# Storing the first tile later and the last tile in two pieces, in a one-core SiLU-times-gate kernel

## Chip, cores, metric

One core of one Trainium2 chip. The metric is device time in microseconds (us); lower is better. Times inside a run are counted from the start of its span, as the profile gives them.

## The reference

The input is `x`, float32 of shape 32 x 512 x 2048. Each row is split in half; the output, 32 x 512 x 1024 float32, is `silu(first half) * second half`:

```python
half_dim = x.shape[-1] // 2
x1, x2 = x[..., :half_dim], x[..., half_dim:]
return (x1 * (1 / (1 + np.exp(-x1))) * x2).astype(np.float32)
```

So 134.2 MB are read and 67.1 MB written, with two operations per output element.

## The kernel before

The 16,384 rows are cut into 16 tiles of 8 rows on each of 128 partitions. Loads go out from SP, stores from ACT, each tile in one transfer: 8.4 MB in, 4.2 MB out. The silu runs on ACT, the product on DVE. Two input and two output buffers. Only the first tile (in chunks of 2 rows) and the last (stored in four pieces of 2 rows) are treated differently.

```python
K = 8
KC_EDGE = 2
# ... pools of 2 buffers each; silu() on ACT and mul() on DVE over rows c to ce ...
def load(i):
    xt = in_pool.tile([P, K, in_cols], dt, name="xt")
    nc.sync.dma_start(out=xt[:, :plan[i][1], :], in_=view(x_flat, i))
    loaded[i] = xt

load(0)
load(1)
for i in range(n_tiles):
    xt = loaded.pop(i)
    ov = view(out_flat, i)
    ot = out_pool.tile([P, K, half], dt, name="ot")
    if i < n_tiles - 1:
        kc = KC_EDGE if i == 0 else K
        for c in range(0, K, kc):
            silu(ot, xt, c, c + kc)
            mul(ot, xt, c, c + kc)
        nc.scalar.dma_start(out=ov, in_=ot)
        if i + 2 < n_tiles:
            load(i + 2)
        continue

    cuts = list(range(0, K, KC_EDGE))
    for n, c in enumerate(cuts + [None, None]):
        if c is not None:
            silu(ot, xt, c, c + KC_EDGE)
            mul(ot, xt, c, c + KC_EDGE)
        if n >= 2:
            b = cuts[n - 2]
            nc.scalar.dma_start(out=ov[:, b:b + KC_EDGE, :], in_=ot[:, b:b + KC_EDGE, :])
```

## Time and profile before

| | before |
|---|---|
| time, median of 3 runs | 470.57 us (470.44 to 471.02) |
| span of the profiled run | 468.6 us |
| DVE / ACT busy | 30% / 24% |
| bytes moved, mean rate | 201.3 MB, 430 GB/s |
| tile 0 done on DVE, store 0 issued | 32.7 us |
| last load lands | 450.65 us |
| store 14 lands; last piece lands | 457.9; 467.7 us |

Read it from the DMA side: the 16 DMA engines (here "engines", where nothing else is said) are busy throughout, and the compute engines wait for them. The lines that show this stand in the prediction.

### The profile page before, as it was taken

How to read it: one execution, taken by the hardware profiler on the slowest of the kernel's cores; microseconds unless marked ns; L12 is line 12 of the kernel's file. 1: busy time of each engine (PE TensorE's matmuls, PEld its weight loads, DVE VectorE, ACT ScalarE, POOL GpSimd, SP SyncE). 2: the span in 40 equal slices, each digit the busy share in tenths (PEclk: the TensorE clock that was granted, in tenths of full speed). 3: DMA queues.
4: the chain of work that ended last, by engine and by line, in shares of the span. 5: the costliest groups of instructions: out<-in, count | busy, mean ns of one | idle time of the engine just before them, and what ended most of it. 6: DMA issues, size and time to landing. Idle time of an engine off the chain costs nothing.

```text
span 468.6 us, 183 instructions
## 1 busy us (share of the span) xinstructions
DVE 139.5 (30%) x22; ACT 114.3 (24%) x23; POOL 0.2 (0%) x4
## 2 busy tenths in 40 slices
DVE  0070510606115060250702407024070330703333
ACT  1141405023050230503205032050410504105050
POOL 0000000000000000000000000000000000000000
DMA  9899999999999998998999999999999999999998
GB/s 442 386 425 403 439 456 448 403 417 434 448 448 403 448 470 380 448 481 380 481 400 420 478 448 403 403 448 448 448 403 445 434 420 448 431 420 492 394 411 358
DMA packets 5040, 201.33 MB, mean 430 GB/s; under 512 B 560, under 2 KB 560, under 8 KB 560
## 3 DMA queue, kind: packets, MB, share of 16 engines
q1 hardware_dynamic: 2304, 134.22, 66.4%
q10 hardware_dynamic: 2736, 67.11, 33.2%
HBM read 134.22 MB, written 67.11 MB: 430 GB/s over the span
## 4 chain that ended last, share of the span: by engine, by line
DMA 72%; DVE 14%; ACT 11%; DVEq 0%; issue 0%; ACTq 0%
DMA xt<-in_x_dram 72%; DVE ot L85 14%; ACT ot L78 11%; DVEq L140 0%; ACTq L78 0%
## 5 line engine op out<-in xcount | busy, mean ns | idle before, releaser
L85 DVE TENSOR_TENSOR ot<-ot,xt 128x8192 f32<-128x8192 f32 (+1 forms) x22 | 139.5, 6362 | 322.1 <-ACT ot L78 322.1
L78 ACT ACTIVATE ot<-xt 128x8192 f32<-128x8192 f32 (+1 forms) x22 | 113.0, 5163 | 343.0 <-DMA xt<-in_x_dram 343.0
L78 ACT ACT_TABLE_LOAD x1 | 1.3, 1283 | 0.8 <-PEq L129 0.8
L129 POOL MEMSET const-bfloat16-1.0<- 128x1 bf16 x1 | 0.1, 101 | 0.0
L129 POOL MEMSET const-uint8-127<- 128x1 uint8 x1 | 0.1, 101 | 0.0
L129 POOL MEMSET const-float32-0.0<- 128x1 f32 x1 | 0.1, 98 | 0.2 <-issue 0.2
L129 POOL MEMSET const-float32-1.0<- 128x1 f32 x1 | 0.1, 98 | 0.0
## 6 DMA issues: line engine op xcount, KB each, us to landing
out_dram<-ot ACTq DMA_DIRECT2D x15, 4096.0 KB, 34.7
out_dram<-ot ACTq DMA_DIRECT2D x4, 1024.0 KB, 5.7
xt<-in_x_dram SPq DMA_DIRECT2D x16, 42.1
```

The costliest lines, as they stand in the source:

```text
L78: nc.scalar.activation(out=ot[:, c:ce, :], in_=xt[:, c:ce, :half], func=mybir.ActivationFunctionType.Silu,)
L85: nc.vector.tensor_mul(out=ot[:, c:ce, :], in0=ot[:, c:ce, :], in1=xt[:, c:ce, half:],)
L129: nc = _bacc.Bacc("TRN2", target_bir_lowering=False, num_devices=1)
```

## The change

Its intent: with tile 0 in chunks of 4, 2 and 2 its store is issued later, so the loads get ahead of the stores; the last tile is then computed sooner and can be stored in two larger pieces without the queue running dry.

```diff
+    KS = 4
+    CHUNKS_FIRST = [4, 2, 2]
@@ tiles 0 to 14
-            kc = KC_EDGE if i == 0 else K
-            for c in range(0, K, kc):
+            c = 0
+            for kc in CHUNKS_FIRST if i == 0 else [K]:
                 silu(ot, xt, c, c + kc)
                 mul(ot, xt, c, c + kc)
+                c += kc
@@ last tile (the old loop over cuts is removed)
+        pieces = []
+        for c in range(0, K, KC_EDGE):
+            silu(ot, xt, c, c + KC_EDGE)
+            if len(pieces) == 1 and c == K - KC_EDGE:
+                nc.scalar.dma_start(out=ov[:, pieces[0]], in_=ot[:, pieces[0]])
+            mul(ot, xt, c, c + KC_EDGE)
+            if (c + KC_EDGE) % KS == 0:
+                pieces.append(slice(c + KC_EDGE - KS, c + KC_EDGE))
+        nc.scalar.dma_start(out=ov[:, pieces[-1]], in_=ot[:, pieces[-1]])
```

More of the change, by code (lines that the diff above doesn't have):

```diff
@@ L105 @@
             continue
-        cuts = list(range(0, K, KC_EDGE))
-        for n, c in enumerate(cuts + [None, None]):
-            if c is not None:
-                silu(ot, xt, c, c + KC_EDGE)
-                mul(ot, xt, c, c + KC_EDGE)
-            if n >= 2:
-                b = cuts[n - 2]
-                nc.scalar.dma_start(out=ov[:, b:b + KC_EDGE, :], in_=ot[:, b:b + KC_EDGE, :])
+        pieces = []
[7 more added lines that the diff above has]
+        nc.scalar.dma_start(out=ov[:, pieces[-1]], in_=ot[:, pieces[-1]])
 _INS = ['x']
```

## The prediction

> **What bounds the kernel now.** I read the page first, for which resource is busy.
>
> ```profile
> span 468.6 us, 183 instructions
> DVE 139.5 (30%) x22; ACT 114.3 (24%) x23; POOL 0.2 (0%) x4
> ...
> DMA  9899999999999998998999999999999999999998
> ...
> q1 hardware_dynamic: 2304, 134.22, 66.4%
> q10 hardware_dynamic: 2736, 67.11, 33.2%
> HBM read 134.22 MB, written 67.11 MB: 430 GB/s over the span
> ```
>
> The reader is to see two engines idle for 70% and more, and a row of nines: the transfers fill the span. q1 (loads) and q10 (stores) together take 99.6% of the 16 DMA engines. Next, the same by stretch, cut at the first load's data, the first store, the last load's landing and the end of the data (the last two columns are DMA share and GB/s):
>
> ```profile
> 2.00:21.80 19.80, 0.00 (x0) 0.06 (x1) 0.00 (x0) 1.00 0.98 424
> ...
> 38.80:450.60 411.80, 121.69 (x14) 98.41 (x14) 0.00 (x0) 1.00 1.00 434
> 450.60:457.90 7.30, 5.23 (x3) 7.17 (x4) 0.00 (x0) 1.00 0.95 410
> 457.90:467.40 9.50, 3.67 (x2) 0.14 (x1) 0.00 (x0) 1.00 0.95 403
> 467.40:468.63 1.23, 0.00 (x0) 0.00 (x0) 0.00 (x0) 1.00 0.00 0
> ```
>
> A packet counts in the window in which it starts, hence the wobble in short ones. Third, the chain of waits, at its start and end:
>
> ```profile
> 44.84 7.04 ACT ot L78
> 51.88 0.02 issue
> 51.90 8.70 DVE ot L85
> 60.61 0.02 issue
> 60.62 42.14 DMA xt<-in_x_dram
> ...
> 450.73 1.92 ACT ot L78
> 452.65 0.02 issue
> 452.67 6.70 DVE ot L85 x3
> 459.37 2.20 DVEq L140
> ```
>
> It alternates ACT 7.04, DVE 8.70 and a load of 42.1 us, and so looks like a dependency loop. It is not one: the load issued at 60.6 stands in the queue behind another that takes the first 13 us, so shortening ACT or DVE would only lengthen its wait. The packet records confirm this: from 1.0 us to the last data at 467.4 no DMA engine pauses, with one exception given below. The end is therefore the start of the data, plus the sum of the packets' times, plus any gap in the feeding.
>
> Fourth, the tail in the timeline:
>
> ```profile
> 450.73 5.51 ACT L78 ACTIVATE ot<-xt 128x2048 f32<-128x2048 f32 x3 [21.93 <-DMA xt<-in_x_dram]
> 452.67 8.90 DVE L85 TENSOR_TENSOR ot<-ot,xt 128x2048 f32<-128x2048 f32 x4 [15.15 <-ACT ot L78]
> 455.00 0.34 ACTq L114 DMA_DIRECT2D out_dram<-ot  x1
> 456.15 1.89 ACT L78 ACTIVATE ot<-xt 128x2048 f32<-128x2048 f32 x1
> 457.20 4.74 ACTq L114 DMA_DIRECT2D out_dram<-ot  x3
> ```
>
> The four pieces of the last store are issued at 455.00, 457.20, 459.4 and 461.6, and take 5.4, 5.6, 5.9 and 6.1 us to land: at 460.4, 462.8, 465.3 and 467.7, a steady 2.44 us apart (1.05 MB in 2.44 us is 430 GB/s). Store 14, issued at 437.56, lands 20.4 us later at 457.9. So the pieces wait behind it, and the queue is full until the last byte. The first piece has 457.0 - 455.0 = 2.0 us of slack before the first engine is done with store 14 (packet records: engines finish it between 456.96 and 457.56).
>
> **What the Trainium skill says.** "DMA: Bandwidth & Descriptors", section "Queues, rings and completion order": each DMA engine goes round-robin between the queue rows that have work, a packet at a time. The trace agrees. Load packets are 65,536 B and take 2.418 us, store packets 32,768 B and take 1.213 us, and they alternate on each engine, which gives 134.22 to 67.11 MB, two to one. The same page, section "Issuing engines are not separate DMA queues", says that transfers from different issuing engines share the same 16 DMA engines; the 66.4% and 33.2% that add to one budget show it. "Perfetto Trace Analysis", section "DMA Instruction — HWDGE (DVE, Sync)", says that the profiled window of such an issue leaves out the data movement: here 0.34 us of issue against 5.4 to 6.1 us to landing. The same page, section "DMA Optimizations", recommends larger transfers for throughput but splitting where some part can then start sooner. The change trades one against the other.
>
> **The change part by part.**
>
> *1. Fewer, larger pieces.* Each engine moves 32 packets of 8,192 B in the tail now: 32 x 0.309 = 9.89 us. It will move 16 packets of 16,384 B. Between 8,192 B (0.309) and 32,768 B (1.213) the line is 0.3013 us per 8 KiB plus 0.008 per packet, so a 16 KiB packet should take 0.610 (an estimate), and 16 of them 9.77. Saved: 0.12 us, and two completion records of 0.01 us: 0.14 us in all. This is on the path that sets the end, because the queue is.
>
> *2. Tile 0 in 4, 2, 2.* Four 128x2048 activations take 7.31 us, one 1.893, one of 128x8192 7.029. By the line between the sizes a 128x4096 one takes 3.61. On DVE 2.286 and 8.692 give 4.42 for 128x4096. Tile 0 lands at 21.83: first silu to 25.44, first mul 25.47 to 29.89, then two of 2 rows at 2.21 apart, the last ending at 34.30. Now it ends at 32.67. Store 0 and load 2 go out 1.63 us later, at 34.33. Load 2 loses nothing, since load 1 keeps the queue busy to 44.8. Store 0 enters the alternation later, so all loads move ahead of the stores. With smooth sharing they would land 1.63/2 = 0.8 us earlier. In truth it goes by packets: an engine either fits in one more load packet before its first store packet, and then every load is ahead by one store packet, 1.21 us, or it does not and nothing moves. Total bytes are unchanged, so this part alone moves the end by 0; its use is to start the last tile's computing sooner.
>
> Which is it? Store 0, issued at 32.70, has its first packet at 38.86 to 39.46, after load packets that began at 33.0 and 35.5. The latter took 3.4 instead of 2.42 us: that is the exception, a 1.0 us pause as the idle store queue wakes. An engine starts a load packet every 2.42 us, so the latest issue that still gets this slot lies somewhere between 32.70 (which got it) and about 34.6 (one packet time later, less the 0.5 us by which the engines differ); where, the records do not say. 34.33 is near the far end, so a shift is likelier than not, but the first load got its data only 1.0 us after its issue, which would put the limit late. I give 60% to the whole shift, 15% to only some engines shifting (a load lands when its slowest engine does, so that is worth little), 25% to none.
>
> *3. The tail's feeding.* The first piece now needs four rows, so it waits for the second mul: 457.20, not 455.00. With the shift it is 457.20 - 1.21 = 455.99. The second and last goes out at 461.61, or 460.40 shifted. From issue to data flowing on idle engines I take the first load: issued at 0, its first packets start at 1.00 to 1.74, but the second ones only at 4.03 to 4.55; less one packet of 2.42, data flow counts as starting 1.6 to 2.1 us after the issue.
> - Shifted: ready at 457.6 to 458.1, against engines that run dry at 456.96 to 457.56. A gap of about 0.5 us; less the 0.14 saved, +0.4 us. The second piece is ready at 460.40 + 2.1 = 462.5, before the first is done at 457.9 + 4.9 = 462.8: no second gap, barely.
> - Not shifted: ready at 458.8 to 459.3, a gap of some 1.8 us, less 0.14: +1.6 to +1.7 us.
>
> The last landing is followed by about 0.9 us of ending that stays.
>
> **The rivals.**
> - *A hidden tail*: the shift happens and a busy queue takes up a new store without a pause. Speaking for it: stores 1 to 14 queue behind one another and no pause shows. Against: they are issued some 5 us before they are needed (store 13 takes 34.7 us to land, of which 29 are its own share), this piece 1 us. Then only -0.14 remains: 470.4.
> - *A bare tail*: no shift, gap in full. For it: 34.33 is close to the old slot. 472.2.
> - *A new buffer wait*: a later store 0 could hold up the output buffer, of which there are two. Store 13 lands at 443.4 and tile 15 starts to write the same buffer at 450.7: 7.3 us of slack. The store is later by 2.4 at most, the load earlier by 1.2: 3.7 us remain. Unlikely.
> - *Compute-bound end*: the last mul ends at 461.6 in both, earlier with the shift, and cannot set the end alone.
>
> **Range and chances.** The time of a run is about 2.0 us above the trace's span, 470.57 against 468.6, which I hold constant. 60% near 471.0 (470.57 + 0.4), 25% near 472.2, the rest between, with the hidden tail at the low side and 0.3 us of run noise (470.44 to 471.02 before): 471.0, range 470.0 to 472.4. Two per cent is 9.4 us, more than any term here; it would take a steady stall that I do not see. Faster 0.5%, same 98.5%, slower 1%.
>
> **What would show each step.** Right: tile 0's last DVE instruction ends near 34.3 and store 0 is issued just after; later loads land 1.2 us earlier than now (load 15 at 449.4 rather than 450.65); the two last issues are 4.4 us apart near 456.0 and 460.4; store 14 still lands near 457.9; the DMA rate between 38.8 and 449 stays 434 GB/s. Wrong: load 15 still at 450.65 (no shift), a pause of over 1 us in the store queue after store 14, a 16 KiB packet that is not near 0.61 us, or ACT waiting for an output buffer. The forecast as a whole fails if the span moves by more than 2 us, which would mean that the alternation itself has a different rhythm.

## More of the kernel before

One more view is needed. A count of the packets that start between 38 and 41 us shows when store 0 gets its turn (columns: packets, MB, share of the 16 engines; q1 is the loads' queue, q10 the stores'):

```profile
DMA packets 32, 1.57 MB, mean 524 GB/s; under 512 B 0, under 2 KB 0, under 8 KB 0
...
q1 hardware_dynamic: 16, 1.05, 80.6%
q10 hardware_dynamic: 16, 0.52, 40.4%
```

All 16 engines start exactly one store packet here. I call this the early slot of store 0.

## The result, and the profile after

| | before, same rounds | changed |
|---|---|---|
| median | 470.66 us (6 runs) | 471.53 us (6 runs) |
| range | 470.44 to 471.02 | 470.42 to 472.30 |
| the runs | 470.57, 471.02, 470.44, 470.56, 470.90, 470.75 | 470.42, 472.30, 472.12, 472.18, 470.62, 470.94 |

A ratio here is the mean time of one kernel's fast runs over the mean of the other's of the same rounds, so not quite the ratio of the medians. It is 1.0015 (95% interval 0.9998 to 1.0033): the same, within 2%. But the changed kernel has two modes: three runs at 470.4 to 470.9 and three at 472.1 to 472.3. All runs are with the clock at 1.0.

The profiled run is the one of 470.42. Its page, against the lines of before in the prediction:

```profile
span 468.5 us, 179 instructions
...
q1 hardware_dynamic: 2304, 134.22, 66.5%
q10 hardware_dynamic: 2448, 67.11, 33.2%
```

Four instructions and 288 store packets fewer (2,736 before), the same bytes, the same span to 0.1 us. The stretches, cut at this run's own marks (last columns: DMA share, GB/s):

```profile
41.30:449.50 408.20, 121.70 (x14) 98.41 (x14) 0.00 (x0) 1.00 1.00 434
449.50:458.00 8.50, 6.43 (x3) 7.31 (x4) 0.00 (x0) 1.00 0.97 418
458.00:467.40 9.40, 2.47 (x2) 0.00 (x0) 0.00 (x0) 1.00 0.94 403
```

The long middle still moves 434 GB/s. The chain of waits and the tail of the timeline:

```profile
43.59 7.04 ACT ot L80
...
50.65 8.70 DVE ot L87
...
59.37 42.20 DMA xt<-in_x_dram
```

```profile
449.63 7.31 ACT L80 ACTIVATE ot<-xt 128x2048 f32<-128x2048 f32 x4 [21.84 <-DMA xt<-in_x_dram]
451.57 8.90 DVE L87 TENSOR_TENSOR ot<-ot,xt 128x2048 f32<-128x2048 f32 x4 [15.05 <-ACT ot L80]
456.10 0.34 ACTq L114 DMA_DIRECT2D out_dram<-ot  x1
460.50 0.34 ACTq L118 DMA_DIRECT2D out_dram<-ot  x1
```

The reader is to see the same rhythm (7.04, 8.70, 42.2), begun 1.25 us earlier: tile 1's silu starts at 43.59 and not 44.84, tile 15's at 449.63 and not 450.73. The first piece goes out at 456.10, while store 14 still occupies the engines until 457.04 to 457.64 by the packet records, and its data follow without a pause. In the records of packets that start between 38 and 41 us there are now

```profile
DMA packets 11, 0.72 MB, mean 240 GB/s; under 512 B 0, under 2 KB 0, under 8 KB 0
...
q1 hardware_dynamic: 11, 0.72, 77.0%
```

no store packets at all. By the packet records store 0's first ones start at 41.36 to 41.98 on all 16 engines: the late slot.

### The profile page after: what moved, and what is told of

Read it like the earlier page. It is cut to its first block, busy times and chain, and to the rows that moved or that the text cites. A ratio compares the mean times of both kernels' runs of the same rounds, so it can differ in the third digit from the quotient of the medians.

```text
span 468.5 us, 179 instructions
## 1 busy us (share of the span) xinstructions
DVE 139.4 (30%) x21; ACT 114.2 (24%) x22; POOL 0.2 (0%) x4
## 4 chain that ended last, share of the span: by engine, by line
DMA 72%; DVE 14%; ACT 11%; DVEq 0%; issue 0%; ACTq 0%
DMA xt<-in_x_dram 72%; DVE ot L87 14%; ACT ot L80 11%; DVEq L144 0%; ACTq L80 0%
## 5 line engine op out<-in xcount | busy, mean ns | idle before, releaser
L87 DVE TENSOR_TENSOR ot<-ot,xt 128x8192 f32<-128x8192 f32 (+2 forms) x21 | 139.4, 6659 | 321.0 <-ACT ot L80 321.0
L80 ACT ACTIVATE ot<-xt 128x8192 f32<-128x8192 f32 (+2 forms) x21 | 112.9, 5400 | 342.0 <-DMA xt<-in_x_dram 342.0
```

The source lines that it names most:

```text
L80: nc.scalar.activation(out=ot[:, c:ce, :], in_=xt[:, c:ce, :half], func=mybir.ActivationFunctionType.Silu,)
L87: nc.vector.tensor_mul(out=ot[:, c:ce, :], in0=ot[:, c:ce, :], in1=xt[:, c:ce, half:],)
```

## The experiments

**The theory.** Store 0 takes one of a few discrete places in the alternation of load and store packets on each engine. Its issue at 34.4 to 34.5 us lies on the edge between two places. In the late slot the loads gain a store packet's time, 1.21 us, the first piece is issued before the engines run dry, and the time is 470.5. In the early slot, on all or some engines, the larger first piece comes too late. **Rival A**: the late store 0 itself costs time in some runs. **Rival B**: the larger pieces have a varying cost of their own. A further question is what the pause of about 1 us before store 0's first packet is.

The first four ran on one chip (before, in the same rounds: median 470.93, 470.46 to 471.90, 7 runs), the next four on a second (before: 471.05, 470.33 to 471.77), the last four on a third (before: 471.19, 470.45 to 471.69, 9 runs). Edits are against the changed kernel unless said otherwise. All results were correct.

**e1_tile0_only: tile 0's part of the change alone.**

```diff
-        pieces = []
-        ... two pieces of 4 rows ...
+        ... four pieces of 2 rows, as before ...
```

> Tile 0 in 4, 2, 2 as in the changed kernel, the last tile stored in four pieces as before. Slot theory (the changed kernel has two modes, near 470.5 and 472.2 us, because store 0 gets its first packet one slot later in some runs and not in others, and only without the later slot do the larger tail pieces leave the DMA engines dry): with small pieces the tail is fed in both slots, so every run lies between 470.3 and 471.1, one mode. Rival A (the late store 0 itself costs time in some runs): runs near 472.2 show up here too. Rival B (the larger tail pieces themselves have a varying cost, whatever tile 0 does): one mode near 470.6 here, two modes in the run with the tail alone.

Measured: 470.59, 471.52, 471.72, 470.57; ratio to before 0.9999 (0.9981 to 1.0018). The profiled run (470.59) has the late slot, loads 1.1 us earlier than before (load 15 at 449.59) and yet no earlier end (last landing 467.87, before 467.71). So moving the loads ahead does not by itself shorten anything, as predicted: bytes are bytes. The expectation of one mode failed: two runs are 1 us slow. They were not profiled; before itself had such runs in these rounds (471.23, 471.70, 471.90), so these runs cannot be charged to the change. One possible reason is found below in e4: a single early engine brings store 14 to land at 459.19, and with before's 9.80 us of data and 0.92 us of ending the span would be 469.9, an estimate from those traces, against 469.7 and 469.9 in these two runs. That is not shown, but it leaves a weak form of rival A open: a lone early engine may cost about 1.1 us with small pieces too.

**e2_tail_only: the tail's part alone.**

```diff
-    CHUNKS_FIRST = [4, 2, 2]
+    CHUNKS_FIRST = [2, 2, 2, 2]
```

> Tile 0 in four chunks of 2 as before, the last tile stored in two pieces of 4 rows. Slot theory: store 0 always has the early slot, so the last load lands near 450.65, the first piece is issued at 457.2 and the engines, dry from 457.0 to 457.6 on, stand for some 1.7 us; all runs between 471.8 and 472.5, one mode, and the profile shows the pause after store 14. Rival A: all runs near 470.5. Rival B: two modes, 470.5 and 472.2, as in the changed kernel.

Measured: 471.52, 471.11, 471.32, 472.18; ratio 1.0009 (0.9988 to 1.0029). No run near 470.5, so rivals A and B are not supported, but three of the four lie below the range that I expected. In the profile store 0 has the early slot, load 15 lands at 450.99 and the first piece goes out at 457.54. The packets that start between 457.0 and 458.3 us:

```profile
DMA packets 13, 0.00 MB, mean 0 GB/s; under 512 B 13, under 2 KB 13, under 8 KB 13
...
q10 hardware_dynamic: 13, 0.00, 0.6%
```

Thirteen completion records (packets of 4 bytes that report a finished transfer) and no data: the engines stand. By the packet records they run dry at 456.9 to 457.9, and the piece's data start at 458.38 to 458.53, that is 0.84 us after its issue, with no further delay. The last piece lands at 468.74, 1.0 us later than before. The pause is real, and smaller than predicted.

**e3_first5: store 0 safely late.**

```diff
-    CHUNKS_FIRST = [4, 2, 2]
+    CHUNKS_FIRST = [5, 3]
```

> Changed kernel with tile 0 in chunks of 5 and 3, which ends tile 0 at about 35.2 to 35.4 us, 0.8 us later than 4, 2, 2. Slot theory: store 0 always has the late slot (first packets near 41.4), the last load lands near 449.5, no pause in the tail; all runs between 470.2 and 470.9, one mode. Rival A: as slow or slower than the changed kernel, runs near 472. Rival B: two modes as in the changed kernel.

Measured: 470.79, 471.05, 470.98, 470.98; ratio 0.9996 (0.9981 to 1.0011). One mode, no run beyond 471.05, though up to 0.15 us above the range given. Store 0 is issued at 35.30, has the late slot on all engines (first packets 41.30 to 41.94), load 15 lands at 449.50, the pieces go out at 456.05 and 460.45, the last landing is 467.69. The tail from store 14's landing is 9.71 us, against 9.80 with four pieces.

**e4_after_again: the changed kernel, to catch the slow mode.** No edit.

> The changed kernel once more, for a profile of its slow mode and for the share of the modes. Slot theory: in a run near 470.5 the first store packets come near 41.4 and load 15 lands near 449.5; in a run near 472.2 they come near 38.9 on all or some engines, load 15 lands near 450.7 and the store queue pauses after store 14 for about 1.7 us. Rivals A and B: slow runs with the same slot of store 0 as fast ones.

Measured: 472.38, 472.44, 472.54, 472.01; ratio 1.0026 (1.0010 to 1.0041). On this chip all four runs are slow, while 5 and 3 beside it never was: means of 472.34 and 470.95. The packets that start between 38 and 41 us:

```profile
DMA packets 14, 0.88 MB, mean 295 GB/s; under 512 B 0, under 2 KB 0, under 8 KB 0
...
q1 hardware_dynamic: 13, 0.85, 97.8%
q10 hardware_dynamic: 1, 0.03, 2.5%
```

One store packet, where before had 16 and the fast mode none: a single engine of the 16 took the early slot. A load has landed when its slowest engine is done, and that engine is now behind the others for the rest of the run: the first of its 16 completion records for load 15 comes at 449.02, the last at 451.94. Against the mean of the other 15 that engine is 2.6 us late: one store packet (1.21), and a second pause that only this engine had (no packet for 0.48 us, then a load packet from 40.70 that took 3.69 in place of 2.42, together 1.75), less 0.35 because its first pause was the shorter one (0.85, the others' mean 1.20). The landing itself is 2.44 us after e3's 449.50. The tail then starts later than in any other mode:

```profile
452.02 7.31 ACT L80 ACTIVATE ot<-xt 128x2048 f32<-128x2048 f32 x4 [21.97 <-DMA xt<-in_x_dram]
453.96 8.90 DVE L87 TENSOR_TENSOR ot<-ot,xt 128x2048 f32<-128x2048 f32 x4 [15.19 <-ACT ot L80]
458.49 0.34 ACTq L114 DMA_DIRECT2D out_dram<-ot  x1
```

and between 457 and 459 us the stores' queue carries next to nothing, where the changed kernel's fast run carried 0.85 MB (first fence: this run, second: the fast one):

```profile
q10 hardware_dynamic: 17, 0.03, 4.2%
```

```profile
q10 hardware_dynamic: 68, 0.85, 99.8%
```

The last piece lands at 469.69, 11.2 us after the first one's issue, as in e2 (468.74 - 457.54). This is the slow mode. Its end, 1.95 us after the fast run's 467.74, has two parts: store 14 itself lands 1.16 us later (459.19, in the fast run 458.03), which has nothing to do with the pieces, and the pause ahead of the larger first piece adds 0.79.

**e5_first3: store 0 a little earlier.**

```diff
-    CHUNKS_FIRST = [4, 2, 2]
+    CHUNKS_FIRST = [3, 3, 2]
```

> Changed kernel with tile 0 in chunks of 3, 3 and 2: store 0 issued near 33.7 us, between the 32.8 (early slot on all 16 engines, seen with the tail alone) and the 34.4 (early on one engine of 16, seen in the slow mode). Slot theory: early slot on all engines or all but a few. All early: load 15 at 450.7 to 451.0, first piece at 457.2 to 457.5, pause of 0.9 to 1.3 us, time near 471.4. Mixed: the last landing of each load is later by about 1.2 us than with all engines alike, first piece near 458.5, time near 472.4. Never 470.5. Rival (the modes are chance of the chip and have nothing to do with when store 0 is issued): the same mixture of 470.5 and 472.3 as the changed kernel.

Measured: 471.40, 471.14, 471.12, 471.05; ratio 1.0002 (0.9987 to 1.0017). As expected for the early slot: issued at 33.59, 15 engines early, one late at 42.07. The one late engine is ahead in the loads and so delays none (load 15 at 450.76). First piece at 457.31, last landing 468.52: again 11.2 us later. The rival (modes by chance of the chip) would have had runs at 470.5 and 472.3; there were none.

**e6_first8: a whole slot later still.**

```diff
-    CHUNKS_FIRST = [4, 2, 2]
+    CHUNKS_FIRST = [8]
```

> Changed kernel with tile 0 in one chunk of 8: store 0 issued near 37.8 us, one packet time of 2.4 us and more after the edge near 34.4. Slot theory: every engine is one slot later than in the fast mode (first store packets near 43.8), load 15 lands near 448.4, no pause in the tail, all runs 470.3 to 471.0 in one mode; a new wait of ACT for the output buffer at tile 15 is possible but of under 0.5 us. Rival (a late store 0 costs time by itself, the store queue being short of work at the start): 1 to 2 us slower than with 5 and 3.

Measured: 471.15, 470.99, 471.12, 471.10; ratio 1.0000 (0.9985 to 1.0015). The first store packets start at 43.61 to 44.32, one 2.4 us slot after e3's, all loads land another 1.0 us earlier (load 15 at 448.47), and nothing is won; three of the four runs lie up to 0.15 us above the range that I expected. The buffer wait that the prediction called unlikely for the change appears here: ACT's waits are now put down to the store that frees the output buffer,

```profile
ACT ot L80 <- DMA out_dram<-ot: 309.0, 14, 23.2
```

because store 13 lands at 448.64, 0.17 us after the load. This is the limit of the direction.

**e7_warm_before: is the pause a queue's first use?** Kernel before, with a small transfer on ACT's queue at the start.

```diff
     load(0)
+    wt = warm_pool.tile([P, 16], dt, name="wt")
+    nc.scalar.dma_start(out=wt, in_=x_flat[0:P, 0:16])
     load(1)
```

> Kernel before, with one small transfer (128 x 64 bytes into an unused tile) issued on ACT's queue at the start, so that this queue has been used when store 0 comes. If the pause of 1.0 us on each engine at store 0's first packet is that of a queue's first use, it vanishes, the span and the time fall by about 0.9 us (469.6). If it comes whenever an idle queue joins a busy one, the packets before store 0 still take 3.3 to 3.5 us in place of 2.42 and the time is as before, 470.5 to 470.8.

Measured: 472.17, 472.46, 472.67, 471.61; ratio 1.0024 (1.0008 to 1.0041). The experiment had a flaw: the helper that moves one transfer ahead of the start barrier took the small one, so load 0 went out at 0.93 us and not 0, and the times say nothing about the pause. The packets do: the load packets before store 0 still take 0.8 to 1.07 us longer on all engines, although the queue had been used. It is not a queue's first use.

**e8_before_again: before's own slow runs.** Kernel before, no edit.

> The kernel before once more, for the profile of one of its runs beyond 471.2 us (three of seven on the last chip). Slot theory: in such a run one or more engines took another slot for store 0 or paused twice, the loads land up to 1.2 us late and the last landing of the stores is about 1 us later; in a run near 470.5 all 16 engines have the same slot. Rival: the same slot on all engines in both kinds of run, and the time lost elsewhere (one engine that runs slower throughout).

Measured: 470.78, 470.68, 470.50, 470.68, beside runs of the very same code at 470.33 to 471.77; ratio 0.9990 (0.9973 to 1.0007). None of the runs beyond 471.2 was caught, so their cause stays open. In the profiled one all 16 engines have the early slot, and the last landing is 467.93 because one engine ends 0.32 us after the next slowest (0.12 in the profile of before). The lesson is the size of the noise: about 1.4 us between runs of one kernel.

**e9_one_queue: no second queue at all.** Kernel before, all stores issued from SP.

```diff
-            nc.scalar.dma_start(out=ov, in_=ot)
+            nc.sync.dma_start(out=ov, in_=ot)
```

(and the same for the four pieces)

> Kernel before with the stores issued from SP, on the loads' own queue, so that no second queue ever joins. If the pause of about 1 us on each engine belongs to an idle queue joining a busy one, no load packet takes over 2.6 us after the first ones, and the whole ends about 1 us sooner: span 467.5 to 467.8, time 469.5 to 469.9, one mode without runs beyond 470.3. Load and store packets no longer alternate but come tile by tile. Rival: the pause is that of the first store packet as such (the change from load to store), then one of 0.8 us and more stands before the first store packet, or even before each store (15 times, 15 us slower).

Measured: median 475.53 (474.43 to 475.80, 5 runs); ratio 1.0091 (1.0077 to 1.0106). The expectation failed. The pause is still there: no packet starts on any engine in the 2.5 us from 38.6 (columns: busy times, DMA share, GB/s; the second line is the end of the run),

```profile
38.60:41.10 2.50, 0.00 (x0) 0.00 (x0) 0.00 (x0) 1.00 0.00 0
...
468.00:472.00 4.00, 0.00 (x0) 0.00 (x0) 0.00 (x0) 1.00 0.23 96
```

because the packets from 37.8 took 0.8 to 1.5 us longer than 2.42. They are the last packets of load 1. What starts behind them, between 41.4 and 42.3 us, is on each engine load 1's completion record and then the first packet of store 0:

```profile
DMA packets 32, 0.52 MB, mean 583 GB/s; under 512 B 16, under 2 KB 16, under 8 KB 16
```

So a joining queue is not the condition, and the first part of the rival came true: the pause stands directly ahead of the first store packet. Nor does it come at a fixed time after the issue. In e2 store 0 was issued at the same time (32.82, here 32.83), and there the pause is in the packets from 35.4, because the first store packets come one load packet earlier. In all 14 profiles the load packet directly ahead of each engine's first store packet is such a long one, by 0.36 to 1.66 us (found by matching the end of each packet with the start of the next). Whether the step from loads to stores causes the pause is not shown.

The kernel is 4 us slower. A pause on all engines before each store, 15 us in all, as the rival had it, did not come. But 46 load packets in the rest of the run take 0.2 to 1.1 us longer, 45 of them directly ahead of a store, on one to seven engines at a time, and the engines drift apart; the 16 completion records of one transfer spread over 4.8 us near the end, against 0.6 before. At the end most engines are done while the slowest still works, hence the 96 GB/s. That this drift makes up the 4 us is read from the trace and was not tested.

**e10_one_queue_2p: the same with two pieces.** As e9, on the changed kernel, with tile 0 in chunks of 2.

```diff
-    CHUNKS_FIRST = [4, 2, 2]
+    CHUNKS_FIRST = [2, 2, 2, 2]
-            nc.scalar.dma_start(...)
+            nc.sync.dma_start(...)
```

> The same, with tile 0 in chunks of 2 and the last tile stored in two pieces of 4 rows. In one queue the last load should land two whole stores before the end, near 447.5, so the first piece is out near 454, before store 14 is done near 457: no pause in the tail although tile 0 is not delayed. 0.1 us faster than with four pieces, 469.4 to 469.8; if the larger pieces cost something of their own, 471 or more.

Measured: 475.28, 475.44, 474.82, 475.82; ratio 1.0090 (1.0077 to 1.0104). The same loss and the same spread of 5.0 us, in any tail. The expected 469.4 to 469.8 failed with e9.

**e11_one_piece: the price of waiting for the data.** Tile 0 in 5 and 3, the last tile stored whole.

```diff
-    KS = 4
-    CHUNKS_FIRST = [4, 2, 2]
+    KS = 8
+    CHUNKS_FIRST = [5, 3]
```

> Tile 0 in 5 and 3, and the last tile stored in one piece of 8 rows. From the runs with a pause in the tail, the last landing was the issue of the first piece plus 0.85 us plus the data's 9.8 plus 0.35. The one piece is issued near 460.45, so the last landing should be at 471.4 and the span at 472.3, time 474.2 to 474.6; store 14 still ends near 458.0. If landing came earlier, the pause would not be what the tail costs.

Measured: 474.86 (one run, state unknown), span 472.5. The piece is issued at 460.62, its data start at 461.47 (0.85 us later), it lands at 471.71, 11.1 us after its issue; store 14 landed at 458.11. The sum of the tail holds to 0.3 us (471.4 expected); the time is 0.26 us above the range given.

**e12_after_third: the changed kernel again.** No edit.

> The changed kernel once more. Every run near 470.5 (all engines in the late slot) or 472.1 to 472.5 (one or a few engines in the early slot, load 15 near 451.9, first piece near 458.5); the profile shows which, and in both cases the last landing is the later of store 14's end plus 9.75 us and the first piece's issue plus 11.2.

Measured: 472.44, 472.57, 470.54, 470.94; ratio 1.0011 (0.9992 to 1.0031). Both modes, on a third chip. The profiled run (472.44) has again exactly one engine early (38.88, the others 41.39 to 41.84), load 15 lands at 451.90, the first piece is issued at 458.45 and the last one lands at 469.65, 11.2 us later.

**Taken together**, the end in every two-queue profile with pieces of 4 rows is the later of two sums: store 14's landing plus 9.71 us of data, or the first piece's issue plus 11.2 us. "Engines early" counts those of the 16 that took the early slot.

| run | store 0 issued | engines early | load 15 lands | first piece issued | store 14 + 9.71 | issue + 11.2 | last landing |
|---|---|---|---|---|---|---|---|
| e2 (2, 2, 2, 2) | 32.82 | 16 | 450.99 | 457.54 | 467.94 | 468.74 | 468.74 |
| e5 (3, 3, 2) | 33.59 | 15 | 450.76 | 457.31 | 467.80 | 468.51 | 468.52 |
| e4 (4, 2, 2) | 34.42 | 1 | 451.94 | 458.49 | 468.90 | 469.69 | 469.69 |
| e12 (4, 2, 2) | 34.44 | 1 | 451.90 | 458.45 | 468.85 | 469.65 | 469.65 |
| changed, profiled (4, 2, 2) | 34.53 | 0 | 449.55 | 456.10 | 467.74 | 467.30 | 467.74 |
| e3 (5, 3) | 35.30 | 0 | 449.50 | 456.05 | 467.69 | 467.25 | 467.69 |
| e6 (8) | 37.68 | 0 | 448.47 | 455.13 | 467.85 | 466.33 | 467.87 |

The chunks 4, 2, 2 put the issue within 0.1 us of the edge: 34.42 and 34.44 gave one early engine, 34.53 (and 34.50 in e1) none. No version beat before: 5 and 3, the best, is its equal (0.9996), without the changed kernel's slow mode. Differences of a few tenths of a microsecond between the times of different kernels say little of their DMA streams: a run's time is 1.8 us above its span in e1 and e10, 1.9 to 2.0 in before, and 2.3 to 2.5 in e3 and e6.

## Why the prediction was right, and where its steps were off

- **The bound.** Right: the engines carry 433 to 436 GB/s from 50 to 440 us in every profile, and no arrangement changed the total by over 0.5% apart from the one-queue runs and the single piece. 471.53 lies in 470.0 to 472.4, near 471.0.
- **The larger pieces.** A 16 KiB packet was put at 0.610 us and takes 0.611. The saving was put at 0.14; it is 0.09 (9.80 to 9.71 from store 14 to the end), and it is lost again to store 14, which lands 0.1 us later. The ending after the last landing, held at 0.9, is 0.92 us with four pieces and 0.79 with two; that is where the span's 0.1 us comes from.
- **Tile 0.** The delay of 1.63 us is right (34.53 after a load 0 that landed 0.2 later). So is the arithmetic of whole packets: in the late slot load 15 is 1.1 us earlier, put at 1.21. The edge between the slots was put between 32.70 and about 34.6; it was passed by one engine at 33.59 (e5) and by the last one between 34.44 and 34.50.
- **Full shift.** Its outcome was wrong, put at +0.4 us and measured at none (470.42; e3's ratio 0.9996). The failing term is "data flow counts as starting 1.6 to 2.1 us after the issue", read from a load on empty engines at the start. A store on dry engines starts in 0.84 us (e2, e11), and the piece issued 0.9 us before need did not pause at all. The rival "hidden tail" described this mode.
- **No shift.** For the same reason its +1.6 was too much: e2 lands 1.0 us later than before.
- **Some engines shift.** This was the step that failed. It was given 15%, set aside as "worth little" and placed between the other two. It is the worst of the three: one early engine in 16 made every load 1.3 us later than before and the run 472.4, and in the six, four and four runs of the changed kernel it is the likely mode of all those at 472.0 and more (two of them profiled). The prediction had half of the reason in hand, that a load lands with its slowest engine, but not the second pause that the lone engine gets (1.75 us in e4, 1.74 in e12). So it is partly luck that the median lies near the forecast: two mis-sized terms went opposite ways, and 471.53 is the middle of two modes, with no run between 470.94 and 472.12.
- **The pause.** Called the idle store queue waking. e7 has it on a queue that had been used, and e9 without a second queue, so e9 refutes that. In every profile it stands directly ahead of each engine's first store packet and moves with it. What it is stays open, and also why a lone engine pauses twice; no run parts the issue of store 0 from that of load 2, which go out together.

## What to carry to other kernels

When the DMA engines never stand still, count what feeds them: splitting and delaying can move work within the stream but wins only the gaps that exist, here none. An issue time that decides an order between queues should lie well clear of the edge (35.3 and not 34.4 us), because one of 16 engines on the other side delays every later transfer. And look at all the runs: a median of 471.53 hid two modes at 470.6 and 472.2.

## What the Trainium skill lacked or had wrong

- "DMA: Bandwidth & Descriptors", section "Queues, rings and completion order", has the round-robin by packet, which the runs confirm, but not that the place of a joining queue is settled per engine and then lasts: store 0 issued at 32.70 us moved its first data at 38.86, at 34.53 only at 41.36, and one engine of 16 in another place delayed all loads by 2.4 us against the even case, to the end of the run.
- The same page, section "Latency and other measured facts", gives some 600 ns to the first byte of transfers issued as here. The stores on dry engines took 0.84 and 0.85 us from issue to the first data packet, the first load of the run 1.00 to 1.74; on busy engines store 0's took 6.2 us before, and 4.4 at the least (e12).
- The same page, section "Issuing engines are not separate DMA queues", says that issuing from several engines saves only issue time. In e9 and e10, moving the stores to the loads' queue cost 0.9% (475.5 and 475.4 us), with the engines' completions 4.8 to 5.0 us apart instead of 0.6. The measurement decides: here two queues were better.
- No page has the pause that each engine makes in the load packet directly ahead of its first store packet, in every profile, by 0.36 to 1.66 us (in before 0.97 to 1.18).
